# Depthwise convolution of a conformer layer: from taps spread over four engines to shifted copies multiplied on TensorE

## The chip, the cores and the metric

One Trainium2 chip, one core of it. The time is device microseconds from the start to the end of the program; the kernel before was run three times. In the profile PE is TensorE's matmul, PEld its weight load, DVE is VectorE, ACT is ScalarE, POOL is GpSimd, SP is SyncE. SPq and ACTq are the instruction streams of SP and ACT where they issue DMA transfers.

## The reference, cut to what matters

The program is four transformer layers over 256 tokens of width 1024, all float32. The second of them (the odd layer of the first block) is a convolution module followed by a mixture of experts. The part that changes is its first half:

```python
u = modulate(x, mix_pre_g, sh_m, sc_m)              # RMS norm, scale, shift: 256 x 1024
a, g = jnp.split(u @ pw1_w + pw1_b, 2, axis=-1)     # first pointwise layer, 1024 -> 2048
h = a * jax.nn.sigmoid(g)
h = depthwise_conv(h, dw_w) + dw_b                  # 31 taps along the tokens, a filter for each channel
h = jax.nn.silu(layernorm(h, ln_g, ln_b))
y = h @ pw2_w + pw2_b                               # second pointwise layer
x = x + gt_m * rmsnorm(y, mix_post_g)
```

The depthwise convolution adds, for each of 1024 channels and 256 tokens, 31 products of a tap with the value some tokens away.

## The kernel before

Weights come from HBM in pieces of 128x1024 floats (512 KB) into raw buffers, loaded by SP in the order of one long plan (class `Stream`). For a float32r product each piece is split into a rounded part and its remainder: ACT writes `hi` (L98), DVE or POOL `lo` (L99). A product is then three passes on PE, hi by hi, lo by hi, hi by lo (`mm3`, L92 to L94). There are 8 raw buffers, 10 more from the start of the second layer on, and 5 buffers each for `hi` and `lo`. The splits run ahead of the products by one chunk (two pieces).

The first pointwise layer is an exception: its 16 pieces are used as they are (`"raw"` in `conv_specs`), as plain float32 weights against the float32 input `Cu`. Channels lie on the partitions, in 8 blocks of 128; a loop of four steps makes two blocks each. For a block, PE makes the value half and the gate half (`ch`, L1059), ACT and DVE the sigmoid by tanh (`csg`, L1063 and L1064), and DVE the gated value with 15 zeros at either end (`chp`, L1068). A shifted tap is then a window of `chp`. Two tables, PE_TAPS and POOL_TAPS, say which engine computes which of the 31 taps: PE multiplies by a diagonal matrix of the tap (`diag`, L1072, built by POOL in layer 0), ACT scales a window and POOL adds it (`ctp` and `cyp`, L1082 and L1083), DVE multiplies and adds in one step (`cy`, L1086). PE turns the sums to tokens on partitions into banks of PSUM (`cyt`, L1072), where DVE takes the statistics for the layer norm (`bn`, L1096); ACT and DVE normalise into `xs` (L1107, L1109), PE turns it back (`czt`, L1119), and the second pointwise layer follows (`pz`). Behind it come a residual, the router and the experts, with weights held back by `st.pause` until the router is done.

The order of the instructions on each engine is fixed when the program is built, by a scheduler that goes by the dependences and its own estimate of times. On the chip each engine but PE's weight loads goes strictly in that order. A DMA transfer signals one of eight semaphores, used in turn by SP's and ACT's transfers, and waits for the transfer that used the same one before.

Of the kernel before, what the change touches and what calls it, by code (L numbers as in the profile page):

```python
# [21 lines left out]
T = 256  # L22
# [217 lines left out]
def rchunk(w, r0):  # L240
# [39 lines left out]
def layout(inputs):  # L280
# [5 lines left out]
    for g, names in GROUPS.items():  # L286
        a[g] = np.ascontiguousarray(np.concatenate([a.pop(k).reshape(-1, 128) for k, _ in names]).T)
    a["lambdas"] = np.concatenate([a.pop("l0_lambda_" + k) for k in ("q1", "q2", "k1", "k2")])
# [703 lines left out]

PE_TAPS = (1, 1, 3, 5, 1, 7, 5, 15)
POOL_TAPS = (13, 15, 13, 12, 11, 13, 10, 4)

LAST = (3, 6, 7)
# [9 lines left out]
def conv_diag(e, dw, pool):  # L1008

    t = pool.tile([128, sum(PE_TAPS), 128], F32, name="diag")  # L1010
    n = 0
    for cb, c in enumerate(PE_TAPS):
        for j in range(c):
            e.nc.gpsimd.tensor_tensor(t[:, n, :], e.ident, dw[:, 8 * j + cb:8 * j + cb + 1].to_broadcast([128, 128]), op=OP.mult)
            n += 1
    return t
# [19 lines left out]
def conv_mix(e, st, u, I, V, dw, diag, bias, banks, wk, wt, done, ps, z):  # L1036
# [3 lines left out]
    y = wk.tile([128, KB, T], F32, name="cy", bufs=1)  # L1040
    ba, bg = V["l1_conv_pw1_b"][:, 0:8], wk.tile([128, KB], F32, name="hbg", bufs=1)
    nc.vector.tensor_scalar(bg, V["l1_conv_pw1_b"][:, 8:16], 0.5, None, op0=OP.mult)
    p = banks.all("cyt")

    p7 = ps.tile([128, 2, 128], F32, tag="tap", name="cyt", bufs=1)
    spots = [[p[tb][cb // 4][:, 128 * (cb % 4):128 * (cb % 4) + 128] if cb < 7 else p7[:, tb, :] for cb in range(KB)]
             for tb in range(2)]
    runs = [[p[tb][0], p[tb][1][:, 0:384], p7[:, tb, :]] for tb in range(2)]
    st6 = wk.tile([128, 2, 3, 6], F32, name="bn", bufs=1)
    for i in range(4):  # L1050
        w = [st.next(), st.next()]
        for f in range(2):
            hs = ps.tile([128, 2, T], F32, tag="mm", name="ch")
            with ExitStack() as c:
                if i == 0 and f:
                    c.enter_context(e.tc.issue_after(last.ins))
                for j in range(2):
                    for k in range(KB):
                        last = nc.tensor.matmul(hs[:, j, :], w[j][k // 4][:, k % 4, 128 * f:128 * f + 128], u[:, k, :],  # L1059
                                                start=(k == 0), stop=(k == KB - 1))  # L1060
            cb = 2 * i + f
            s = wt.tile([128, T], F32, tag="csg", name="csg")
            nc.scalar.activation(s, hs[:, 1, :], AF.Tanh, bias=bg[:, cb:cb + 1], scale=0.5)  # L1063
            nc.vector.tensor_scalar(s, s, 0.5, 0.5, op0=OP.mult, op1=OP.add)  # L1064
            h = wt.tile([128, T + 2 * PAD], F32, tag="chp", name="chp", bufs=3)
            nc.gpsimd.memset(h[:, 0:PAD], 0.0)
            nc.gpsimd.memset(h[:, PAD + T:], 0.0)
            nc.vector.scalar_tensor_tensor(h[:, PAD:PAD + T], hs[:, 0, :], ba[:, cb:cb + 1], s, op0=OP.add, op1=OP.mult)  # L1068
            tap = lambda j: dw[:, 8 * j + cb:8 * j + cb + 1]
            yb = y[:, cb, :]  # L1070
            n0, n1 = PE_TAPS[cb], PE_TAPS[cb] + POOL_TAPS[cb]
            mm = lambda tb, *m, start=False, stop=False: nc.tensor.matmul(spots[tb][cb], *m, start=start, stop=stop,  # L1072
                                                                          skip_group_check=True)
            for j in range(n0):
                for tb in range(2):
                    mm(tb, h[:, 128 * tb + j:128 * tb + j + 128], diag[:, sum(PE_TAPS[:cb]) + j, :],
                       start=(j == 0 and (cb in (0, 4) or cb == 7 and tb == 0)))
            yp = wt.tile([128, T], F32, tag="cyp", name="cyp")
            nc.scalar.activation(yp, h[:, n0:n0 + T], AF.Identity, bias=V["l1_conv_dw_b"][:, cb:cb + 1], scale=tap(n0))
            for j in range(n0 + 1, n1):  # L1080
                t = wt.tile([128, T], F32, tag="ctp", name="ctp", bufs=4)
                nc.scalar.activation(t, h[:, j:j + T], AF.Copy, scale=tap(j))  # L1082
                nc.gpsimd.tensor_tensor(yp, yp, t, op=OP.add)  # L1083
            nc.vector.tensor_scalar(yb, h[:, n1:n1 + T], tap(n1), None, op0=OP.mult)
            for j in range(n1 + 1, TAPS):
                nc.vector.scalar_tensor_tensor(yb, h[:, j:j + T], tap(j), yb, op0=OP.mult, op1=OP.add)  # L1086
            parts = [yb, yp]
            if cb < 6:
                nc.vector.tensor_tensor(yb, yb, yp, op=OP.add)
                parts = [yb]  # L1090
            for tb in range(2):
                for q in parts:
                    mm(tb, q[:, 128 * tb:128 * tb + 128], e.ident, stop=(q is parts[-1]))
                if cb in LAST:
                    k = LAST.index(cb)
                    nc.vector.bn_stats(st6[:, tb, k, :], runs[tb][k])  # L1096
# [7 lines left out]
    for c, cs in enumerate((slice(0, 512), slice(512, 896), slice(896, 1024))):  # L1104
        for tb in range(2):
            if tb != (c == 2):
                nc.scalar.activation(z[:, tb, cs], runs[tb][c], AF.Identity, bias=nm[:, tb:tb + 1], scale=r[:, tb:tb + 1])  # L1107
            else:
                nc.vector.tensor_scalar(z[:, tb, cs], runs[tb][c], mv[:, tb, 0:1], r[:, tb:tb + 1],  # L1109
                                        op0=OP.subtract, op1=OP.mult)  # L1110
# [808 lines left out]
class Model:  # L1919
# [187 lines left out]
    def consts1(self, work):  # L2107
# [5 lines left out]
        load_cols(e, self.V, self.I, "vd", q, e.nc.scalar)  # L2113
        self.diag = conv_diag(e, self.V["l1_conv_dw_w"], q)
# [8 lines left out]
    def odd(self):  # L2123
# [6 lines left out]
        with ExitStack() as c2:  # L2130
# [3 lines left out]
            dw, diag, bias = V["l1_conv_dw_w"], self.diag, self.bias  # L2134
            wtc = ExitStack()
            wt = wtc.enter_context(tc.tile_pool(name="wkt", bufs=2))
            U = wt.tile([128, KB, T], F32, name="Cu", bufs=1)
            banks = Banks(psy)
            g, sh = self.gain(mod[1, 0][:, 8:16], V["l1_mix_pre_g"], "gc"), mod[1, 0][:, 0:8]
            for tb in range(2):  # L2140
# [3 lines left out]
            with tc.issue_after(act.ins):  # L2144
                gtb = self.gate_row(mod[1, 1][:, 0:8], V["l1_mix_post_g"], wk, "gtb")
# [180 lines left out]
```

## Time and profile before

| | |
|---|---|
| median of 3 runs | 1992.06 us (1989.18 to 1993.62) |
| profiled execution | 2003.04 us, its span 2001.3 us |
| PE busy | 1834.0 us, 92% |
| DVE busy | 1590.6 us, 79% |
| ACT busy | 1192.3 us, 60% |
| POOL busy | 520.9 us, 26% |
| granted TensorE clock, mean | 0.942 |
| HBM read | 465.10 MB, 233 GB/s over the span |

The span is from the first to the last instruction, the profiled time also has what lies around it. A share of the whole span is a mean over stages with different bounds, so the stage with the convolution (about 580 to 696 us) has to be read by itself. [...] One plain float32 product on PE shows as two records.

### The profile page before, as it was taken

The numbers are of one execution on the slowest core, as the hardware profiler recorded it, in microseconds if no ns is written. First come the engines' busy times: TensorE is split into PE (matmuls) and PEld (weight loads), VectorE is DVE, ScalarE is ACT, GpSimd is POOL, SyncE is SP. The second block draws the span as 40 slices with busy tenths as digits, with TensorE's granted clock in tenths as the row PEclk, the third lists the DMA queues.
The fourth block names the chain that finished last, engine by engine and source line by source line (L and its number), as shares of the span: only waits on it lengthen the run. The fifth ranks groups of instructions, "written<-read, shape, count | busy, mean of one in ns | idle before, by whom it ended". The sixth has DMA issues, their size and how long they took to land. (4 is left out here: it accounts for less than half of the span.)

```text
span 2001.3 us, 33220 instructions
## 1 busy us (share of the span) xinstructions
PE 1834.0 (92%) x12339; PEld 1636.7 (82%) x12339; DVE 1590.6 (79%) x2343; ACT 1192.3 (60%) x1844; POOL 520.9 (26%) x460
## 2 busy tenths in 40 slices
PE   6789988699998679999999999999999689989997
PEld 3678677689976569999999999999998689878896
DVE  5887898677559858999999999999998595569555
ACT  5455455455445447777777777777776544345443
POOL 1645564533227631000000000000000433335051
PEclk9889899799999889999999999999999789889799
DMA  9846676289763227999999999999996232233220
GB/s 362 286 163 211 211 229 234 81 314 322 247 215 106 79 85 268 368 347 333 348 365 349 333 350 362 353 333 345 367 350 232 95 116 96 69 126 133 81 75 22
DMA packets 132463, 468.41 MB, mean 234 GB/s; under 512 B 14994, under 2 KB 16274, under 8 KB 132292
## 3 DMA queue, kind: packets, MB, share of 16 engines
q1 hardware_dynamic: 131008, 464.38, 65.0%
q8 instruction: 99, 1.62, 0.3%
q10 hardware_dynamic: 1172, 1.65, 0.2%
q14 instruction: 72, 0.59, 0.1%
q0 software_dynamic: 112, 0.17, 0.1%
HBM read 465.10 MB, written 1.05 MB: 233 GB/s over the span
## 5 line engine op out<-in xcount | busy, mean ns | idle before, releaser
L99 DVE TENSOR_TENSOR lo<-raw,hi 128x1024 fp32r<-128x1024 f32 x678 | 858.1, 1281 | 137.2 <-ACT hi L98 112.7
L98 ACT CAST hi<-raw 128x1024 fp32r<-128x1024 f32 x718 | 746.3, 1048 | 298.3 <-PE ph L94 92.4
L93 PE MATMUL ph<-lo,gh 128*128 128x256 f32 x1408 | 396.5, 282 | 3.5 <-DVE lo L99 1.7
L94 PE MATMUL ph<-hi,gl 128*128 128x256 f32 x1408 | 396.2, 282 | 0.0
L92 PE MATMUL ph<-hi,gh 128*128 128x256 f32 x1408 | 393.7, 280 | 0.0
L93 PEld LDWEIGHTS ph<-lo,gh 128*128 128x128 f32 x1408 | 264.2, 188 | 12.6 <-DVE lo L99 6.8
L94 PEld LDWEIGHTS ph<-hi,gl 128*128 128x128 f32 x1408 | 264.2, 188 | 3.4
L92 PEld LDWEIGHTS ph<-hi,gh 128*128 128x128 f32 x1408 | 264.4, 188 | 2.8
L343 POOL TENSOR_TENSOR adac<-adac,raw 128x512 f32<-128x512 f32 x112 | 196.9, 1783 | 173.5 <-ACT raw L341 100.0
L1613 POOL MEMSET kv<- 64x2 f32 x4 | 0.4, 97 | 790.3 <-DVE lo L99 773.7
L99 POOL TENSOR_TENSOR lo<-raw,hi 128x1024 fp32r<-128x1024 f32 (+1 forms) x40 | 97.4, 2443 | 158.6 <-ACT hi L98 149.5
L93 PE MATMUL pe<-lo,hhi 128*128 128x512 f32 x352 | 137.8, 392 | 0.0
L92 PE MATMUL pe<-hi,hhi 128*128 128x512 f32 x352 | 136.8, 396 | 0.5 <-ACT hhi L98 0.5
L94 PE MATMUL pe<-hi,hlo 128*128 128x512 f32 x352 | 125.8, 392 | 0.0
L94 PE MATMUL ht<-hi,Hl 128*128 128x256 f32 (+1 forms) x384 | 115.1, 300 | 0.0
L92 PE MATMUL ht<-hi,Hh 128*128 128x256 f32 (+1 forms) x384 | 114.5, 298 | 0.6 <-ACT u L459 0.6
L93 PE MATMUL ht<-lo,Hh 128*128 128x256 f32 (+1 forms) x384 | 114.6, 298 | 0.0
L92 PE MATMUL ph<-Fh,hi 128*128 128x256 f32 x352 | 101.4, 290 | 11.5 <-DVE h L980 8.9
L93 PE MATMUL ph<-Fl,hi 128*128 128x256 f32 x352 | 101.1, 288 | 0.0
L94 PE MATMUL ph<-Fh,lo 128*128 128x256 f32 x352 | 100.1, 287 | 0.0
L1083 POOL TENSOR_TENSOR cyp<-cyp,ctp 128x256 f32<-128x256 f32 x83 | 72.4, 883 | 36.4 <-ACT ctp L1082 32.8
L92 PEld LDWEIGHTS ph<-Fh,hi 128*128 128x128 f32 x352 | 68.2, 195 | 14.5 <-DVE h L980 9.1
(598 smaller groups left out, 4115.9 us busy)
## 6 DMA issues: line engine op xcount, KB each, us to landing
raw<-in_l_moe_w SPq DMA_DIRECT2D x528, 512.0 KB, 5.4
raw<-in_l_mod_w SPq DMA_DIRECT2D x96, 512.0 KB, 5.4
raw<-in_l_ffn_w SPq DMA_DIRECT2D x66, 512.0 KB, 4.5
raw<-in_w_in SPq DMA_DIRECT2D x60, 512.0 KB, 3.6
raw<-in_w_ada SPq DMA_DIRECT2D x32, 512.0 KB, 5.0
raw<-in_l_w_in SPq DMA_DIRECT2D x28, 512.0 KB, 4.9
raw<-in_l_conv_pw_w SPq DMA_DIRECT2D x24, 512.0 KB, 4.5
raw<-in_w_ada SPq DMA_DIRECT2D x32, 256.0 KB, 3.7
```

Source lines behind the costliest of these rows:

```text
L92: mm(out, a[0], b[0], start=start, stop=False, **kw)
L93: mm(out, a[0], b[1], start=False, stop=False, **kw)
L94: return mm(out, a[1], b[0], start=False, stop=stop, **kw)
L98: nc.scalar.copy(hi, src)
L99: (lo_eng or nc.vector).tensor_tensor(lo, src, f32(hi), op=OP.subtract)
L343: nc.gpsimd.tensor_tensor(a[:, 1, i:i + 512], a[:, 1, i:i + 512], y[:, i:i + 512], op=OP.add)
L1083: nc.gpsimd.tensor_tensor(yp, yp, t, op=OP.add)
L1613: nc.gpsimd.memset(kv[64:128, :, T - 1:T], 0.0)
```

## The change

The split among engines is gone. The first pointwise layer's weights are split like all others and multiplied in three passes against a split input (`Ch`, `Cl`). That input is made by `modulate_tb`, which the other layers use already: ACT copies each group of four transposed blocks out of PSUM, DVE casts it and subtracts; the intermediate goes into the buffer `cy` through a small class `Parts`.

For the convolution each block's `chp` (now with 15 and 17 zeros) is copied within SBUF by 16 transfers issued by ACT: for each of four groups `c` of 32 channels and each of four shifts `s`, the 32 partitions of group `c` go to the partitions 32s to 32s+31 of a tile `cx4`, shifted by `s` tokens (32x284 floats, 36 KB). One product with K of 128 then adds four taps of 32 channels: the weights `cD` are 128x32, four diagonal matrices one below the other. Eight such products in a row, each shifted by four tokens, make the 32 taps (the last is zero), and the four groups write to their own 32 rows of one PSUM tile `cc`. POOL builds `cD` from a table of taps laid out on the host and four stacked identities. ACT copies `cc` out with the bias added (`cy`), PE turns it (`cyt`), ACT copies that to `xs`, and the statistics are taken there in four parts. The convolution of a pair of blocks (`convolve`) is written after the next pair's pointwise product.

```diff
 def conv_specs(pw1, pw2):
-        s += [(kchunk(pw1[4 * j + i])[0], "raw") for j in range(2)]
+        s += [kchunk(pw1[4 * j + i]) for j in range(2)]
...
+def conv_taps(e, I, pool):
+    t = pool.tile([128, 256], F32, name="taps")
+    nc.scalar.dma_start(t, I["taps"])
+    d = pool.tile([128, 32], F32, name="id4")
...
+    def convolve(i, xs):
+        p = banks.tile([128, 2, T], F32, name="cc")
+        for f, (x, d) in enumerate(xs):
+            for a in range(8):
+                for c in range(4):
+                    nc.tensor.matmul(p[32 * c:32 * c + 32, f, :], d[:, 8 * c + a, :], x[:, c, 4 * a:4 * a + T],
+                                     start=(a == 0), stop=(a == 7), skip_group_check=True)
+            nc.scalar.activation(y[:, 2 * i + f, :], p[:, f, :], AF.Identity, bias=V["l1_conv_dw_b"][:, 2 * i + f:2 * i + f + 1])
+        q = banks.tile([128, 2, T], F32, name="cyt")
+        for f in range(2):
+            for tb in range(2):
+                nc.tensor.transpose(q[:, tb, 128 * f:128 * f + 128], y[:, 2 * i + f, 128 * tb:128 * tb + 128], e.ident)
+        nc.scalar.copy(z[:, :, 256 * i:256 * i + 256], q)
+        for tb in range(2):
+            nc.vector.bn_stats(st6[:, tb, i, :], q[:, tb, :])
+
+    pend = None
     for i in range(4):
-        w = [st.next(), st.next()]
+        hs = [ps.tile([128, 2, T], F32, tag="mm", name="ch") for _ in range(2)]
+        for j in range(2):
+            w = st.next()
+            for k in range(KB):
+                for f in range(2):
+                    e.mm3(hs[f][:, j, :], w(k, 128 * f, 128), (u[0][:, k, :], u[1][:, k, :]), start=(k == 0), stop=(k == KB - 1))
+        if pend:
+            convolve(*pend)
...
+            d = wt.tile([128, 32, 32], F32, tag="cD", name="cD", bufs=2)
+            nc.gpsimd.tensor_tensor(d, taps[1][:, None, :].to_broadcast([128, 32, 32]),
+                                    taps[0][:, 32 * cb:32 * cb + 32, None].to_broadcast([128, 32, 32]), op=OP.mult)
...
+            h = wt.tile([128, T + 32], F32, tag="chp", name="chp", bufs=3)
...
+            x = wt.tile([128, 4, n], F32, tag="cx4", name="cx4", bufs=3)
+            for s in range(4):
+                for c in range(4):
+                    nc.scalar.dma_start(x[32 * s:32 * s + 32, c, :], h[32 * c:32 * c + 32, s:s + n])
+            xs.append((x, d))
+        pend = i, xs
+    convolve(*pend)
...
             for tb in range(2):
-                for k in range(0, KB, 4):
-                    p = banks.tile([128, 4, 128], F32, name="pt")
-                    act = modulate_bank(e, self.xs, tb, k, g, sh, p, U[:, k:k + 4, 128 * tb:128 * tb + 128], k == 0)
+                last = modulate_tb(e, self.xs, tb, g, sh, U, Parts(y, 512), lambda: banks.tile([128, 1, 512], F32, name="pt")[:, 0, :])
```

ACT's order from the first gated value (`csg`) on, before; `cyp` and `ctp` are the scaled windows that POOL adds:

```order
L1063 ACTIVATE csg<-ch,hbg 128x256
L1079 ACTIVATE cyp<-chp,vc,vd 128x256
L1082 ACTIVATE ctp<-chp,vd 128x256 x10
L1063 ACTIVATE csg<-ch,hbg 128x256
L1082 ACTIVATE ctp<-chp,vd 128x256 x2
L1079 ACTIVATE cyp<-chp,vc,vd 128x256
```

And now, from the same place to the second pair's first copies:

```order
L1076 ACTIVATE csg<-ch,hbg 128x256
L98 CAST hi<-raw 128x1024
L1076 ACTIVATE csg<-ch,hbg 128x256
L1085 DMA cx_5708<-chp 32x284 x16
L1085 DMA cx_5734<-chp 32x284 x16
L98 CAST hi<-raw 128x1024
L1050 ACTIVATE cy<-cc,vc 128x256
L1076 ACTIVATE csg<-ch,hbg 128x256 x2
L98 CAST hi<-raw 128x1024 x3
L1085 DMA cx_5957<-chp 32x284 x6
L1050 ACTIVATE cy<-cc,vc 128x256
L1085 DMA cx_5957<-chp 32x284 x5
```

The scaled windows are gone; in their place 32 transfers stand in a row in ACT's stream, with one weight split, the copy of the convolved block and the next pair's tanh behind them. The 16 pieces of the first pointwise layer are numbers 0 to 15 of these splits: the three ahead of the first row here are 5 to 7, then come 8, 9 (behind the transfers) and 10 to 12, with four pieces to a pair.

PE's order where the second pair's product ends and the first pair's convolution begins, now:

```order
L94 MATMUL ch<-Ch,lo 128x256
L1048 MATMUL cc<-cx_5708,cD 32x256 x32
L1048 MATMUL cc<-cx_5734,cD 32x256 x32
L1054 MATMUL cyt<-ident,cy 128x128 x2
L92 MATMUL ch<-Ch,hi 128x256
```

A block's 32 products stand together, and the next pair's product is behind both blocks of the pair before.

DVE's order at the end of layer 0, before, in the residual that leads to the changed stage (`rt`, `x`, `xs`):

```order
L927 TENSOR_TENSOR rt<-py,gtb 128x512 x2
L84 TENSOR_SCALAR r1v<-r1s 128x1
L927 TENSOR_TENSOR rt<-py,gtb 128x512
L931 SCALAR_TENSOR_TENSOR x<-rt,r1y,x 128x512 x2
L927 TENSOR_TENSOR rt<-py,gtb 128x512
```

The same place now, with the same steps under their new line numbers:

```order
L99 TENSOR_TENSOR lo<-raw,hi 128x1024
L929 TENSOR_TENSOR rt<-py,gtb 128x512 x2
L84 TENSOR_SCALAR r1v<-r1s 128x1
L929 TENSOR_TENSOR rt<-py,gtb 128x512
L372 TENSOR_TENSOR mod_1_676<-bg,vc 128x8
L933 SCALAR_TENSOR_TENSOR x<-rt,r1y,x 128x512 x2
L376 TENSOR_SCALAR mod_1_676<-mod_1_676 128x8
L99 TENSOR_TENSOR lo<-raw,hi 128x1024
L929 TENSOR_TENSOR rt<-py,gtb 128x512
L84 TENSOR_SCALAR r1v<-r1s 128x1
L99 TENSOR_TENSOR lo<-raw,hi 128x1024
```

Three subtractions of weight splits stand in and around the residual now, where there were none; the three copies of the same splits stand on ACT beside it. The order of the expert stage is as before; in the feed-forward part of layer 0 and in the last two layers some instructions have changed places.

## Rows read from the trace of the kernel before

**Rows 1.** Timeline of PE, start of the stage.
```profile
580.83 8.73 PE L1059 MATMUL ch<-Cu,raw 128*128 128x256 f32 x30
...
589.83 6.21 PE L1059 MATMUL ch<-Cu,raw 128*128 128x256 f32 x28
```

**Rows 2.** Timeline, end of the stage: start us, us, instruction.
```profile
693.33 0.39 PE L1072 MATMUL cyt<-ident,cyp 128*128 128x128 f32 x2
693.75 0.30 DVE L1096 BATCH_NORM_STATS2 bn<-cyt 128x6 f32<-128x128 f32 x1 [0.53 <-PE cyt L1072]
...
696.38 0.63 PE L1119 MATMUL czt<-ident,xs 128*128 128x128 f32 x4 [2.67 <-ACT xs L1107]
```

**Rows 3.** Busy us of PE, PEld, DVE, ACT, POOL; granted clock, DMA share, GB/s, by stretch.
```profile
592.00:680.00 88.00, 64.60 (x315) 55.39 (x314) 86.97 (x129) 47.31 (x97) 66.91 (x88) 0.91 0.38 126
680.00:696.00 16.00, 12.84 (x95) 12.46 (x94) 11.16 (x27) 3.16 (x7) 6.64 (x6) 0.87 0.00 0
765.00:1500.00 735.00, 731.56 (x5212) 682.81 (x5211) 687.73 (x748) 568.84 (x694) 1.67 (x1) 1.00 0.96 351
```

**Rows 4.** Costliest groups, 580 to 696 us: count, busy us, mean ns, idle before.
```profile
L1086 DVE SCALAR_TENSOR_TENSOR cy<-chp,vd,cy 128x256 f32<-128x256 f32 x111 | 73.5, 696 | 1.1
L1083 POOL TENSOR_TENSOR cyp<-cyp,ctp 128x256 f32<-128x256 f32 x83 | 72.4, 883 | 36.4 <-ACT ctp L1082 32.8
```

**Rows 5.** Timeline of ACT, start of the stage.
```profile
578.56 1.50 ACT L459 ACTIVATE Cu<-pt,mod,gc 128x128 f32<-128x128 f32 x4 [1.28 <-PE pt L453]
...
590.51 0.48 ACT L1063 ACTIVATE csg<-ch,hbg 128x256 f32<-128x256 f32 x1
```

**Rows 6.** One tile's subtractions: ns min/median/max, first and last start.
```profile
L99 DVE TENSOR_TENSOR cTl<-cs,cTh x4: 683/689/693, 700.0 to 711.1; 128x512 fp32r<-128x512 f32 x4
```

**Rows 7.** Page, part 5: splits of weights, count, busy us, mean ns.
```profile
L99 DVE TENSOR_TENSOR lo<-raw,hi 128x1024 fp32r<-128x1024 f32 x678 | 858.1, 1281 | 137.2 <-ACT hi L98 112.7
L98 ACT CAST hi<-raw 128x1024 fp32r<-128x1024 f32 x718 | 746.3, 1048 | 298.3 <-PE ph L94 92.4
...
L99 POOL TENSOR_TENSOR lo<-raw,hi 128x1024 fp32r<-128x1024 f32 (+1 forms) x40 | 97.4, 2443 | 158.6 <-ACT hi L98 149.5
```

**Rows 8.** Timeline of PE in layer 0's feed-forward part.
```profile
506.88 0.28 PE L93 MATMUL ph<-Fl,hi 128*128 128x256 f32 x1
507.00 0.28 PE L94 MATMUL ph<-Fh,lo 128*128 128x256 f32 x1
507.20 1.06 PE L357 MATMUL adap<-adac,ones 128*32 128x512 f32 x6
508.19 0.50 PE L92 MATMUL py<-hi,hhi 128*128 128x512 f32 x1
```

**Rows 9.** Stretch of the stage's start, columns as in rows 3.
```profile
581.00:592.00 11.00, 11.00 (x46) 9.31 (x45) 1.42 (x5) 2.94 (x8) 0.00 (x0) 0.82 0.95 372
```

**Rows 10.** Timeline of DVE, start of the stage.
```profile
591.02 0.29 DVE L1064 TENSOR_SCALAR csg<-csg 128x256 f32<-128x256 f32 x1 [9.44 <-ACT csg L1063]
591.42 0.48 DVE L1068 SCALAR_TENSOR_TENSOR chp<-ch,vc,csg 128x256 f32<-128x256 f32 x1
```

**Rows 11.** Timeline of ACT, its first two transfers.
```profile
0.80 0.89 ACTq L1906 DMA_DIRECT2D x<-in_x  x2
```

**Rows 12.** Line L1603, issue ns min/median/max, and landing.
```profile
L1603 ACTq DMA_DIRECT2D cw<-in_cmp_w x4: 482/570/1672, 1565.6 to 1787.1; - x4
...
DMA to landing us min/median/max: 1.9/2.0/2.2
```

**Rows 13.** Line L164, the weight loads: issue ns, and landing.
```profile
L164 SPq DMA_DIRECT2D raw<-in_l_moe_w x528: 327/328/702, 580.1 to 1516.0; - x176
...
DMA to landing us min/median/max: 2.6/5.2/11.0
```

**Rows 14.** Timeline of PE, four 32-row products of 256 columns.
```profile
565.84 0.63 PE L357 MATMUL adap<-adac,ones 128*32 128x256 f32 x4
566.39 0.50 PE L92 MATMUL py<-hi,hhi 128*128 128x512 f32 x1
```

More of the change, by code (lines that the diff above doesn't have):

```diff
@@ L287, in layout @@
         a[g] = np.ascontiguousarray(np.concatenate([a.pop(k).reshape(-1, 128) for k, _ in names]).T)
+    w = np.concatenate([a.pop("l1_conv_dw_w"), np.zeros((1, D), np.float32)])
+    a["taps"] = np.ascontiguousarray(w.reshape(8, 4, 8, 4, 32).transpose(1, 4, 2, 3, 0)).reshape(128, 256)
     a["lambdas"] = np.concatenate([a.pop("l0_lambda_" + k) for k in ("q1", "q2", "k1", "k2")])
@@ L989 @@
 PAD = 15
-PE_TAPS = (1, 1, 3, 5, 1, 7, 5, 15)
-POOL_TAPS = (13, 15, 13, 12, 11, 13, 10, 4)
-LAST = (3, 6, 7)
 def conv_specs(pw1, pw2):
@@ L1003, in conv_specs @@
     for i in range(4):
-        s += [(kchunk(pw1[4 * j + i])[0], "raw") for j in range(2)]
+        s += [kchunk(pw1[4 * j + i]) for j in range(2)]
     return s + [rchunk(pw2, 256 * i) for i in range(4)]
[L1008 to L1016, printed above, removed]
+def conv_taps(e, I, pool):
+    nc = e.nc
+    t = pool.tile([128, 256], F32, name="taps")
+    nc.scalar.dma_start(t, I["taps"])
+    d = pool.tile([128, 32], F32, name="id4")
+    nc.gpsimd.tensor_tensor(d, e.ident[:, 0:32], e.ident[:, 32:64], op=OP.add)
+    for i in (64, 96):
+        nc.gpsimd.tensor_tensor(d, d, e.ident[:, i:i + 32], op=OP.add)
+    return t, d
 def conv_bias(e, I, pool, work):
@@ L1033, in conv_bias, with conv_mix @@
     return one, b
-def conv_mix(e, st, u, I, V, dw, diag, bias, banks, wk, wt, done, ps, z):
+def conv_mix(e, st, u, I, V, taps, bias, banks, wk, wt, done, ps, z, y):
     nc = e.nc
-    y = wk.tile([128, KB, T], F32, name="cy", bufs=1)
     ba, bg = V["l1_conv_pw1_b"][:, 0:8], wk.tile([128, KB], F32, name="hbg", bufs=1)
     nc.vector.tensor_scalar(bg, V["l1_conv_pw1_b"][:, 8:16], 0.5, None, op0=OP.mult)
[L1043 to L1049, printed above, removed]
-    for i in range(4):
-        w = [st.next(), st.next()]
-        for f in range(2):
[L1053 to L1060, printed above, removed]
@@ L1067, in conv_mix @@
             nc.gpsimd.memset(h[:, PAD + T:], 0.0)
[L1068 to L1096, printed above, removed]
+            nc.vector.scalar_tensor_tensor(h[:, PAD:PAD + T], hs[f][:, 0, :], ba[:, cb:cb + 1], s, op0=OP.add, op1=OP.mult)
@@ L1103, in conv_mix @@
     nc.vector.scalar_tensor_tensor(nm, mv[:, :, 0], -1.0, r, op0=OP.mult, op1=OP.mult)
-    for c, cs in enumerate((slice(0, 512), slice(512, 896), slice(896, 1024))):
+    for cs in (slice(0, 512), slice(512, 1024)):
         for tb in range(2):
-            if tb != (c == 2):
-                nc.scalar.activation(z[:, tb, cs], runs[tb][c], AF.Identity, bias=nm[:, tb:tb + 1], scale=r[:, tb:tb + 1])
-            else:
-                nc.vector.tensor_scalar(z[:, tb, cs], runs[tb][c], mv[:, tb, 0:1], r[:, tb:tb + 1],
-                                        op0=OP.subtract, op1=OP.mult)
+            if tb:
+                nc.scalar.activation(z[:, tb, cs], z[:, tb, cs], AF.Identity, bias=nm[:, tb:tb + 1], scale=r[:, tb:tb + 1])
+            else:
+                nc.vector.tensor_scalar(z[:, tb, cs], z[:, tb, cs], mv[:, tb, 0:1], r[:, tb:tb + 1], op0=OP.subtract, op1=OP.mult)
     py = banks.all("pz")
@@ L2112, in consts1 @@
         self.moe = Moe(e, self.I, p)
-        load_cols(e, self.V, self.I, "vd", q, e.nc.scalar)
-        self.diag = conv_diag(e, self.V["l1_conv_dw_w"], q)
+        self.taps = conv_taps(e, self.I, q)
         self.bias = conv_bias(e, self.I, q, work)
@@ L2133, in odd @@
             ps = c2.enter_context(tc.tile_pool(name="psc", bufs=2, space=PSUM))
-            dw, diag, bias = V["l1_conv_dw_w"], self.diag, self.bias
+            taps, bias = self.taps, self.bias
             wtc = ExitStack()
             wt = wtc.enter_context(tc.tile_pool(name="wkt", bufs=2))
-            U = wt.tile([128, KB, T], F32, name="Cu", bufs=1)
+            U = tuple(wt.tile([128, KB, T], F32R, name=n, bufs=1) for n in ("Ch", "Cl"))
             banks = Banks(psy)
             g, sh = self.gain(mod[1, 0][:, 8:16], V["l1_mix_pre_g"], "gc"), mod[1, 0][:, 0:8]
+            y = wk.tile([128, KB, T], F32, name="cy", bufs=1)
             for tb in range(2):
-                for k in range(0, KB, 4):
-                    p = banks.tile([128, 4, 128], F32, name="pt")
-                    act = modulate_bank(e, self.xs, tb, k, g, sh, p, U[:, k:k + 4, 128 * tb:128 * tb + 128], k == 0)
-            with tc.issue_after(act.ins):
+                last = modulate_tb(e, self.xs, tb, g, sh, U, Parts(y, 512), lambda: banks.tile([128, 1, 512], F32, name="pt")[:, 0, :])
+            with tc.issue_after(last[0].ins):
                 gtb = self.gate_row(mod[1, 1][:, 0:8], V["l1_mix_post_g"], wk, "gtb")
             st.pause(self.moe_start + 3)
-            py, room = conv_mix(e, st, U, I, V, dw, diag, bias, banks, wk, wt, wtc.close, ps, self.xs)
+            py, room = conv_mix(e, st, U, I, V, taps, bias, banks, wk, wt, wtc.close, ps, self.xs, y)
             residual(e, x, py, gtb, wk, "r2", self.xs, room)
```

12 lines of the change are left out of this document (10 added, 2 removed), and 1 row of the table GROUPS.

## The prediction

> **What bounds the kernel now.** I read the busy times by stretch first, then the costliest groups and the waits of the one stretch that the change rewrites, then its two ends in the timeline. The changed stage begins at 580.83 us with the first pointwise product [rows 1] and ends at 696.38 us, when PE starts turning the normalised result [rows 2]. In between VectorE is the bound: busy 87.0 of 88.0 us from 592 to 680, while PE has 64.6 and ScalarE 47.3 [rows 3]. The groups say with what: 111 tap steps of 696 ns on DVE, 73.5 us, beside 83 additions on POOL for another 72.4 us [rows 4]. DMA moves nothing from 680 to 696, so the weight buffers of the expert stage are full before the stage is over. From 765 to 1500 the expert stage is then full on both PE (731.6 of 735) and DMA (351 GB/s) [rows 3]. Hence every microsecond by which 696.38 moves shows in the total: the transfers ahead are as far as the buffers let them be either way, and no stage behind has room to take it up.
>
> **What goes.** All tap work on DVE, POOL and ACT, and with it the bound; PE's 38 diagonal taps go too. Late next is a chain through three engines, so the new end has to be built step by step, on the clock of the trace before. I call the four steps of the loop pairs 0 to 3 (two blocks of 128 channels each).
>
> **The start.** The modulated input is now copied by ACT alone, four groups of 1.50 us from 578.56 [rows 5], each followed on DVE by a cast and a subtraction; a 128x512 subtraction takes 0.69 us [rows 6], and I take the cast at the same. The first products read the third group: 578.56 + 4.50 + 1.38 = 584.4. Three weight splits now stand between the residual's steps. They cost nothing if they fill its gaps, and 3 x (1.05 + 1.28) = 7.0 us if none does [rows 7]; I take 2, since DVE and ACT alternate there. Start: 586.5, against 580.83.
>
> **The pointwise product.** One pair is 96 float32r passes (2 x 8 x 2 x 3) at 0.12 us [rows 8], 11.5 us. [...] Pair 0 ends at 586.5 + 13.6 = 600.1. Then tanh (0.48) on ACT, two steps on DVE (0.29 + 0.48) [rows 5, 10] and 0.3 to hand on: the first block's copies can be issued at 601.7. Pair 1's product starts at 602.5, when both accumulators are read, and ends at 614.0.
>
> **The copies.** Sixteen transfers of 36 KB a block, all issued by ACT, 32 a pair, 128 in all. This is the step with the widest price. ACT's two transfers of [rows 11] take 0.89 us together, 0.45 each; the four 32 KB ones of [rows 12] have an issue of 0.48 to 1.67, median 0.57; a weight load's issue on SP is down to 0.33 [rows 13]. I take 0.45, the only pair that ACT issued with nothing else between, and keep 0.33 and 0.60 as bounds. A 32 KB transfer lands after 1.9 to 2.2 us, median 2.0 [rows 12]. Every transfer waits for the one eight places earlier, and 8 x 0.45 = 3.6 us is more than 2.0, so that wait is covered; it ceases to be when landing takes over 3.6, as the weight loads do (5.2 median, [rows 13]). Pair 0: 32 x 0.45 = 14.4, issued by 616.1, landed by 618.1.
>
> **The taps on PE.** A block is 8 steps of four products, each into its own 32 rows. Four such products of 512 columns took 0.99 us to the next instruction (507.20 to 508.19), with different data each [rows 8]; of 256 columns 0.55 us [rows 14]. In a stream the step is thus between 0.44 (the difference) and 0.55; I take 0.47, so 3.8 us a block (3.5 to 4.4).
>
> **One round.** Pair 0's first block: 614.0 to 617.8. Its second waits for its copies: 618.1 to 621.9. On ACT stand in a row, behind the 32 issues: one weight split (1.05), the copy out of the first block (0.45), two tanh (0.96), then 1.2 of DVE, so pair 1's copies start 2.8 us after the first block's end: 620.6. They take 14.4, plus 1 us in which the copy of the transposed result, placed among them, waits for PE, plus 2.0 to land: a round of 2.8 + 17.4 = 20.2 us from first block to second block of the next pair. PE's own path is 3.8 + 11.5 + 0.5 + 3.8 = 19.6. The two are nearly equal; the copies lead by 0.6. The weights come in time: a pair's third and fourth splits stand ahead of its copies, only the second half of the pair after next is behind them. The splits add 16 x 1.28 on DVE and 16 x 1.05 on ACT [rows 7], with DVE otherwise nearly empty. POOL builds the tap weights, 128x1024 each, at about 2.4 us (the nearest is its subtraction [rows 7]); two are ready beforehand and the others have a round each.
>
> **The end.** The first blocks end at 617.8, 637.7 and 657.6; the last copies start at 660.4, are issued at 675.8 and landed at 677.8. PE then has nothing but the last two blocks: the first runs from 670.6 to 676.5 (3.8 + 2.1 for the clock), the second from 677.8 to 681.6. Behind it: copy with bias (0.65), transposes (0.35), copy and statistics (2.0), then the unchanged 2.3 us from the last statistics (694.05) to 696.38 [rows 2]. Sum 3.0 + 2.3 = 5.3: 686.9, against 696.38, so 9.5 us earlier. The 38 diagonals that POOL no longer builds in layer 0, and the reordering of some instructions in the last two layers, I put at +0.5 together, between -3 and +3. Net -9.
>
> The profiled execution took 2003.04 us, 1.74 around its span of 2001.3. So the sum is 2003.04 - 9 = 1994, and the median of the three runs stands 10.98 lower: 1992.06 - 9 = **1983 us**.
>
> **Rivals.**
> 1. *ACT's issue becomes the bound* (0.25). If one issue costs 0.60, nearer to the median of [rows 12], pair 0's copies end at 620.9, a round on ACT is 32 x 0.60 + 1 + 3.7 = 23.9, the last copies start at 672.4 and land at 694.6, and the end is 703.7: 7 us later, 1999; with the full 7 us of splits at the start 2004. By straight line the sign turns at 0.53 us an issue. For it: the 1.67 of [rows 12], issued while weights were loading. Against it: only about four weight loads fall into each round.
> 2. *The gain is lost at the start* (0.13). Splits, cast and cold clock put the first product at 593, and the reordered later stages add a little: 1990, no change.
> 3. *The four products of a step run one after another* (0.02), so the change does not do what it says. A block costs 15.2, and the end is 614.0 + 4 x 30.4 + 2 x 12 + 5.3 = 765: 2061. [rows 8, 14] speak plainly against it.
> 4. *Small transfers do not overlap* (0.02). At 2.0 us each, one after another, four pairs take 4 x 64 + 3 x 3.7: an end near 878, 2174. Against it: 512 KB weight loads land after 5.2 us but follow at 351 GB/s, one in 1.5 us [rows 3, 13], so several are under way at once. [...]
> 5. *The issues hide* (0.02), because ACT's issuing runs beside its computing. At nothing an issue, the last copies land at 661.8, right behind pair 2, and the end is 661 + 7.6 + 5.3 = 674: 22 us early, 1970. Against it: in [rows 11] the issues follow one another, 0.89 us for two, and here 32 stand in line with nothing long to hide under. [...]
>
> **How the numbers follow.** My forecast has 0.56, with its own range 1978 to 1988: at an issue of 0.33 the end is 13.3 us early, and 15 with no cost for the splits (1977). To 1974 with all small terms on the good side, and up to 2003, which takes in rival 2 and most of rival 1, leaves under 2 in 10 outside (rivals 3 to 5, the worst of rival 1). A measurement here tells 0.2%, 4 us, from no change. Faster by more: 0.53 of mine, 0.03 of rival 2, 0.01 of rival 1, 0.02 of rival 5: 0.59. Within: 0.03 + 0.08 + 0.03 = 0.14. Slower: 0.21 + 0.02 + 0.04 = 0.27.
>
> **What would show it.** ACT's 128 issues about 0.45 us apart with no wait between them; four products of a step starting together, steps 0.47 apart; first blocks some 20 us apart; a pause on PE of 8 to 10 us before the last pair; the turn of the normalised result at 687. I am wrong if the issues are over 0.53 apart, or if they stop for weight loads; then ACT's queue, not PE, is where the splits and copies stand late.

## The result and the profile after

The change makes the kernel slower: 2011.03 us median (2002.48 to 2032.53, 20 runs) against 1996.82 us (1987.66 to 2004.24, 20 runs), ratio 1.0087 with a 95% interval of 1.0066 to 1.0108. The forecast was 1983 us, 9 us faster, from the 1992.06 of the first three runs of before. (The ratios are taken from undisturbed runs alone, so they are not the quotient of the medians.) The profiled execution took 2021.83 us, its span 2019.9 us.

The stretches of [rows 3] in the changed kernel, with the same columns:

```profile
592.00:680.00 88.00, 64.61 (x685) 57.37 (x684) 22.74 (x35) 19.62 (x30) 12.23 (x16) 0.88 0.43 128
680.00:706.00 26.00, 13.97 (x133) 7.99 (x134) 2.04 (x8) 2.09 (x4) 0.70 (x1) 0.79 0.12 33
```

DVE has gone from 87.0 of 88 us to 22.7, POOL from 66.9 to 12.2. ACT's busy time fell too, from 47.3 to 19.6, and PE's is the same. No engine is the bound by its busy time, and yet the stage ends later. What fills it is not counted as busy: in the 88 us ACT spends 65.0 on issuing copies, beside its 19.6. ACT's timeline shows it; ACTq is ACT where it issues transfers, and in brackets stands its idle time before the row:

```profile
593.03 0.48 ACT L1076 ACTIVATE csg<-ch,hbg 128x256 f32<-128x256 f32 x1
593.08 21.52 ACTq L1085 DMA_DIRECT2D cx<-chp  x32
614.63 1.04 ACT L98 CAST hi<-raw 128x1024 fp32r<-128x1024 f32 x1 [21.12 <-DMA cx<-chp]
615.59 0.47 ACT L1050 ACTIVATE cy<-cc,vc 128x256 f32<-128x256 f32 x1
615.96 0.83 ACT L1076 ACTIVATE csg<-ch,hbg 128x256 f32<-128x256 f32 x2
```

The 32 copies of the first pair take ACT 21.5 us, and the split, the copy of the convolved block and the next pair's tanh come only then. The line of the copies by itself (ns of one issue, min, median, max; then first and last start, and who waited):

```profile
L1085 ACTq DMA_DIRECT2D cx<-chp x128: 514/602/1623, 593.1 to 693.9; - x128
...
  POOL chp L1079: 55.7, 5
  ACT hi L98: 47.3, 3
  ACT cy L1050: 16.7, 1
  ACT xs L1055: 10.3, 2
  PE cc L1048: 6.0, 1
...
DMA to landing us min/median/max: 1.8/1.9/6.6
```

An issue takes 0.602 us, and from one start to the next it is 0.641 (median of the 127 distances). Landing takes 1.9 us, as forecast from [rows 12]. The stage's end on PE:

```profile
683.12 7.12 PE L1048 MATMUL cc<-cx,cD 128*32 128x256 f32 x64 [6.03 <-DMA cx<-chp]
695.17 1.29 PE L1048 MATMUL cc<-cx,cD 128*32 128x256 f32 x6 [4.93 <-ACT cy L1050]
...
705.86 1.14 PE L1110 MATMUL czt<-ident,xs 128*128 128x128 f32 x4 [3.41 <-DVE xs L1101]
```

Before each of its last two blocks PE stands idle for 6.0 and 4.9 us, and the blocks then run at a granted clock of 0.63 and 0.73. These are means, as is the 0.79 of the stretch: the trace records the clock as 0.50 or 1.00 of full speed. The normalised result is turned at 705.86, against 696.38 [rows 2].

To see where the rest of the time went, every traced kernel is cut at the same products. "FFN 0" is the feed-forward part of layer 0 (first `ph` to last `py`), "start" from there to the first pointwise product `ch`, "stage" from it to the first `czt`, "experts" from the first expert product `ph` to the last `pe`, "last layers" from there to the last `hy`. All in us.

| kernel | FFN 0 | start | stage | experts | last layers |
|---|---|---|---|---|---|
| before | 210.9 | 8.6 | 115.6 | 793.8 | 442.7 |
| before, second trace (e12) | 210.8 | 8.6 | 113.0 | 795.8 | 435.1 |
| changed | 202.4 | 16.5 | 128.2 | 797.8 | 448.2 |
| e1: copies issued by SP | 199.2 | 16.5 | 120.2 | 798.4 | 439.9 |
| e2: copies on DVE | 198.7 | 16.5 | 98.3 | 797.8 | 445.3 |
| e3: three passes, old taps | 211.1 | 14.0 | 133.7 | 797.3 | 448.8 |
| e4: new taps, raw weights | 199.1 | 12.1 | 128.5 | 798.4 | 435.8 |
| e6: copies through HBM | 199.8 | 16.5 | 90.4 | 797.8 | 439.6 |
| e7: half as many transfers | 199.7 | 16.6 | 92.0 | 798.4 | 440.1 |
| e8: copies on DVE and ACT | 202.4 | 16.5 | 88.1 | 797.3 | 454.6 |
| e9: changed, diagonals built again | 200.3 | 16.5 | 128.0 | 797.9 | 430.2 |
| e10: e8, order at the experts' head | 205.1 | 16.5 | 88.6 | 797.5 | 441.7 |
| e11: before without the diagonals | 205.6 | 8.5 | 113.6 | 798.5 | 439.3 |

Between the first and the third row the program loses 12.7 us in the stage, 8.0 at the start and 3.9 in the experts, and wins 8.5 in FFN 0: +16.1 us. Ahead of FFN 0 stand 2.6 us less, behind the stage 0.3. The last layers add 5.6 between these two traces, but that can't be put down to the change. The changed kernel, e2, e6, e7, e8 and e9 have the same order of instructions there, and need 430 to 455 us. What differs is the clock that PE was granted in that execution (columns as in [rows 3]; first e9, then the changed kernel, then e8). The kernel before, in its own order, fits in: 435.1 us at 0.92 and 442.7 at 0.90.

```profile
1559.80:1989.90 430.10, 396.64 (x2868) 356.08 (x2868) 287.65 (x734) 198.13 (x434) 155.55 (x100) 0.93 0.29 94
```
```profile
1560.17:2008.41 448.24, 415.46 (x2869) 372.83 (x2868) 287.44 (x734) 198.66 (x434) 154.17 (x100) 0.89 0.28 90
```
```profile
1519.36:1973.91 454.55, 424.04 (x2868) 379.88 (x2868) 287.87 (x734) 198.83 (x434) 155.51 (x100) 0.86 0.28 89
```

### The profile page after: what moved, and what is told of

It reads as the page before. It is cut to its first block, busy times and chain, and to the rows that moved or that the text cites. A ratio compares the mean times of both kernels' runs of the same rounds, so it can differ in the third digit from the quotient of the medians.

```text
span 2019.9 us, 34046 instructions
## 1 busy us (share of the span) xinstructions
PE 1844.9 (91%) x12803; PEld 1645.2 (81%) x12803; DVE 1523.0 (75%) x2234; ACT 1173.2 (58%) x1788; POOL 455.2 (23%) x351
## 5 line engine op out<-in xcount | busy, mean ns | idle before, releaser
L99 DVE TENSOR_TENSOR lo<-raw,hi 128x1024 fp32r<-128x1024 f32 x694 | 871.3, 1271 | 186.4 <-ACT hi L98 166.4
L98 ACT CAST hi<-raw 128x1024 fp32r<-128x1024 f32 x734 | 762.4, 1048 | 319.3 <-PE ph L94 98.9
L92 PEld LDWEIGHTS ht<-hi,Hh 128*128 128x128 f32 x384 | 79.0, 206 | 3.5 <-issue 1.7
L93 PEld LDWEIGHTS ht<-lo,Hh 128*128 128x128 f32 x384 | 78.8, 205 | 1.7 <-issue 1.5
```

Source lines behind the costliest of these rows:

```text
L92: mm(out, a[0], b[0], start=start, stop=False, **kw)
L93: mm(out, a[0], b[1], start=False, stop=False, **kw)
L98: nc.scalar.copy(hi, src)
L99: (lo_eng or nc.vector).tensor_tensor(lo, src, f32(hi), op=OP.subtract)
```

## The experiments

**e1: who issues.** 

```diff
-                    nc.scalar.dma_start(x[32 * s:32 * s + 32, c, :], h[32 * c:32 * c + 32, s:s + n])
+                    nc.sync.dma_start(x[32 * s:32 * s + 32, c, :], h[32 * c:32 * c + 32, s:s + n])
```

> The 128 copies are issued by SP instead of ACT; nothing else is edited. Theory 1 (the changed kernel is late because ACT issues a copy every 0.64 us, 82 us in one line, with its casts and activations standing in that line; an issue costs less on SP, 0.33 us as a weight load's does): the copies of a pair take about 12 us, PE's own path sets the rounds (11.3 + 7.6 + 0.5 = 19.4 us), the normalised result is turned near 667 instead of 705.9, and the time is near 1972. Rival A (the 0.64 us belongs to this kind of transfer, 32 partitions within SBUF, on whatever queue): SP issues at 0.64 too, pairs follow one another every 20.5 us, the turn comes near 685, the time near 1991. Rival B (not the issue but the landing or the shared semaphores pace the copies): they come as late as from ACT, 2011. Rival C (the loss is not in this stage but in the later stages, whose order changed): the stage gets shorter and the time still stays above 2000.

2009.03 us, ratio to before 1.0085 (1.0045 to 1.0125). The copies' line on SP:

```profile
L1085 SPq DMA_DIRECT2D cx<-chp x128: 507/589/1622, 589.5 to 682.4; - x128
```

SP needs 0.589 us an issue, 0.633 from start to start, though it issues its weight loads in 0.33 [rows 13]. So Theory 1's "an issue costs less on SP" fell and rival A's price is right: it belongs to the kind of transfer. Rival B is out by the spacing: eight issues take 8 x 0.633 = 5.1 us, and a copy lands after 1.9 us in the median, so neither landing nor a shared semaphore paces the row. A's time was not reached. The stage is only 8 us shorter, because the copies still stand in one line, 92.9 us from the first start to the last, now with weight loads and their waits between them. In the median even those 8 us don't show, though the interval has room for them.

**e2: no transfers at all, DVE copies.**

```diff
-                    nc.scalar.dma_start(x[32 * s:32 * s + 32, c, :], h[32 * c:32 * c + 32, s:s + n])
+                    nc.vector.tensor_scalar(x[32 * s:32 * s + 32, c, :], h[32 * c:32 * c + 32, s:s + n], 1.0, None, op0=OP.mult)
```

> No transfers: each of the 128 copies of 32x284 is one instruction on DVE (multiply by 1.0), which writes to another group of 32 partitions. Theory 1 (ACT's line of issues sets the stage): a copy should take about 0.3 us (the nearest row is 0.287 us for 128x256 of the same operation), 32 of them 9.6 us a pair, with four weight splits 14.5 us, less than PE's 19.4; PE sets the rounds, the turn comes near 667 and the time near 1972. Rival B (PE's products or the splits set the stage): the turn stays near 700, 2005 to 2011. Rival C (the loss lies in the later stages): the stage gets shorter but the time stays above 2000. A miss of another kind: if a copy to other partitions costs 0.7 us, DVE has 27 us a pair and the gain is gone.

1982.53 us, ratio 0.9926 (0.9895 to 0.9957): faster than before. One line's instructions, and the stretch from the first to the last convolution, with the columns of [rows 3]:

```profile
L1085 DVE TENSOR_SCALAR cx<-chp x128: 295/300/2062, 597.4 to 671.5; 32x284 f32<-32x284 f32 x128
```
```profile
604.00:676.00 72.00, 63.86 (x758) 49.27 (x750) 64.54 (x143) 19.80 (x28) 13.66 (x14) 0.98 0.29 96
```

A copy on DVE takes 0.300 us where its transfer took 0.641 of ACT's line. The stage fell by 30 us to 98.3, not to the some 89 of Theory 1 (a turn near 667). DVE is busy 64.5 of 72 us and some of its copies take up to 2.06, but PE is at 63.9 too; that DVE is the bound here is tested by e8. Rival B is refuted, and C: the stage does reach the total. Twelve of a block's 16 copies write to another group of 32 partitions than they read; their median with the other four, 0.300 us for 284 columns, is near the 0.29 us that the same operation took for 256 columns on their own partitions [rows 10].

**e3 and e4: each part alone.** e3 is the kernel before with

```diff
-        s += [(kchunk(pw1[4 * j + i])[0], "raw") for j in range(2)]
+        s += [kchunk(pw1[4 * j + i]) for j in range(2)]
...
+                    e.mm3(hh[f][:, j, :], w(k, 128 * f, 128), (u[0][:, k, :], u[1][:, k, :]), start=(k == 0), stop=(k == KB - 1))
```

and the split input (and one buffer fewer for the scaled windows, which no run tests by itself); e4 is the changed kernel with these lines and the input as they were before.

> One part of the change alone: the first pointwise layer in three float32r passes with split weights and input, on the old convolution by taps on four engines (one buffer fewer for the scaled windows, for room). Theory 1: the old taps keep DVE the bound, and 16 subtractions of 1.28 us come on top, with cast and subtraction of the input ahead: 20 + 4 us longer, near 2020. Rival (the passes save PE time that counts, 11.3 us a pair against 14.2): faster than before, 1985 to 1990.

> The other part alone: the new convolution with its 128 transfers on ACT, the first pointwise layer with its raw float32 weights and float32 input as before the change. Theory 1 (the line of issues on ACT sets the stage): without weight splits in ACT's line a round is 20.5 + 3 us, and PE's 14.2 + 7.6 + 0.5 = 22.3 lies under it; the start is some 5 us earlier without the split of the input; the turn near 694, the time 1997 to 2001, faster than the changed kernel by about 12 us. Rival B (PE or the splits set the stage): PE's longer product makes it slower than the changed kernel, 2015 to 2020. Rival C (the order of later stages): no clear difference from 2011.

e3: 2032.93 us, ratio 1.0187 (1.0153 to 1.0221). Theory 1's mechanism holds: the stage grows by 18.2 us, near the 20.5 that 16 subtractions cost on DVE [rows 7], the start by 5.4. Its 2020 was 13 us short; in the trace the rest is in the other columns of the table and in the time before FFN 0 (6.0 us). e4: 2005.22 us, ratio 1.0056 (1.003 to 1.0083). The gain over the changed kernel is some 6 us by the medians, half of what was expected, and the two intervals overlap. In the traces the start is 4.4 us shorter (12.1 against 16.5), but the stage is as long as before the undoing: the issues are again 0.642 us apart, and where splits were taken out of ACT's line its waits for PE's longer product grew, from 8.7 us to 14.3. So neither part helps alone, and the three passes cost less inside the new stage than beside the old taps.

**e6 and e7: is it paid per transfer?** e6 goes through HBM in five transfers a block. e7 copies 64 rows at a time and leaves out that the rows belong in other places.

```diff
+    dr = e.ctx.enter_context(e.tc.tile_pool(name="hdp", bufs=3, space=bass.MemoryType.DRAM))
...
-            for s in range(4):
-                for c in range(4):
-                    nc.scalar.dma_start(x[32 * s:32 * s + 32, c, :], h[32 * c:32 * c + 32, s:s + n])
+            hd = dr.tile([128, T + 32], F32, tag="hd", name="hd", bufs=3)
+            nc.scalar.dma_start(hd, h)
+            for s in range(4):
+                nc.sync.dma_start(x[32 * s:32 * s + 32, :, :], hd[:, s:s + n].rearrange("(c p) n -> p c n", c=4))
```
```diff
-            for s in range(4):
+            for s in (0, 2):
                 for c in range(4):
-                    nc.scalar.dma_start(x[32 * s:32 * s + 32, c, :], h[32 * c:32 * c + 32, s:s + n])
+                    nc.scalar.dma_start(x[32 * s:32 * s + 64, c, :], h[64 * (c // 2):64 * (c // 2) + 64, s:s + n])
```

> A block's 16 transfers become five: ACT writes the 128x288 block to a scratch buffer in HBM, SP reads it back four times, once for each shift, 32x4x284 (128 rows) a time. Question: is the 0.64 us of an issue paid per transfer or per row? Theory 1 (per transfer, so 40 issues instead of 128, about 26 us on two queues, and some 4 us a block to write and land): the stage, 128.2 us in the changed kernel from first pointwise product to the turn of the normalised result, comes down to 95 to 102 us, the time to 1978 to 1985. Rival (per row: a read of 128 rows costs four times 0.6): 32 x 2.4 = 77 us on SP, the stage stays at 120 to 128, the time at 2005 to 2011.

> As the changed kernel, on ACT, but half as many transfers of twice the rows: 8 a block of 64x284, same bytes. It leaves the placement of the copies out: a transfer takes 64 neighbouring rows with one shift, so taps meet wrong rows. Theory 1 (an issue costs 0.64 us whatever its rows): 64 issues, 41 us in all instead of 82, a pair's copies 10.3 us; the stage 100 to 105 us instead of 128.2, the time 1985 to 1990. Rival (a cost per row or per byte): each issue about 1.2 us, the stage and the time as in the changed kernel, 2011.

e6: 1977.24 us, ratio 0.9911 (0.9877 to 0.9945). e7: 1987.9 us, ratio 0.9942 (0.9904 to 0.9979). Issue times, first e6's writes and reads, then e7's copies:

```profile
L1085 ACTq DMA_DIRECT2D hd<-chp x8: 326/326/363, 597.8 to 650.9; - x8
```
```profile
L1087 SPq DMA_DIRECT2D cx<-hd x32: 303/430/496, 600.1 to 656.1; - x32
...
DMA to landing us min/median/max: 2.6/3.8/5.4
```
```profile
L1085 ACTq DMA_DIRECT2D cx<-chp x64: 468/607/1122, 588.8 to 654.4; - x64
```

0.602 us for 32 rows, 0.607 for 64: paid per transfer, not per row. e6's copies to and from HBM are cheaper to issue, 0.326 and 0.430 us with 128 rows, though that is no rule for all such copies (the loads of [rows 12] had a median of 0.57). Why the kinds differ no run here shows. Theory 1 is confirmed by both stages (90.4 and 92.0 us, shorter than it said), though e6's copies land later (3.8 us) and need two steps. The rivals, a cost per row or per byte, are out. Against the changed kernel e6 gained 37.8 us of stage with 40 issues instead of 128, e7 36.2 with 64; what they saved was the issuing engine's time, not landing (3.8 and 2.3 us in the median, against 1.9).

**e8 and e10: is PE next?** e8 divides e2's copies, 10 of a block to DVE and 6 to ACT. e10 adds to e8 the old order at the head of the experts; the lines that hand on `m.last`, the last split of the gathered tokens, and read `st.late` are left out here.

```diff
+                    o, v = x[32 * s:32 * s + 32, c, :], h[32 * c:32 * c + 32, s:s + n]
+                    if 4 * s + c < 10:
+                        nc.vector.tensor_scalar(o, v, 1.0, None, op0=OP.mult)
+                    else:
+                        nc.scalar.copy(o, v)
```
```diff
-                oh = m.onehots(0, x)
+                with tc.issue_after(m.last[1].ins) if x else ExitStack():
+                    oh = m.onehots(0, x)
...
+            st.late = range(self.moe_start + 2, self.moe_start + 4), m.last
```

> No transfers; of a block's 16 copies DVE makes 10 (0.30 us each, as measured when DVE made all) and ACT 6. With all on DVE the stage was 98.3 us and DVE was busy 64.5 of its 72 us between first and last convolution. Theory 1 (DVE is the bound there, and PE's 19.4 us a pair comes next): the stage gets to 87 to 90 us, the time to 1971 to 1975. Rival (PE's path is already what sets it): 98, 1982, no change. Second rival (ACT's copies come late, behind its casts): over 98.

> The kernel with copies on DVE and ACT, and two issue orders at the head of the expert stage put back to what they were before the change: ACT's third to sixth weight split, and the second pair's one-hot rows on DVE, behind the last split of the gathered tokens. From the first expert product to the first turned hidden block it took 11.7 us before and 17.6 to 18.8 in all kernels with the change. Theory (in the new order POOL's subtraction starts while DVE still has one-hots and subtractions to do, and two of them take 2.6 us instead of 0.42): 11 to 14 us there, the whole stretch to the end of the experts 793 to 795 instead of 797.4, the time 4 us lower, near 1976. Rival (it comes from weights that arrive later): 17 to 19 as before.

e8: 1980.15 us, ratio 0.9883 (0.9837 to 0.9929). Its stretch from the first to the last convolution:

```profile
604.00:665.00 61.00, 55.69 (x720) 41.66 (x718) 43.42 (x87) 33.13 (x62) 13.83 (x13) 0.99 0.33 105
```

The stage is 88.1 us, where Theory 1 put it, so DVE was e2's bound. PE is now busy 55.7 of 61 us at a clock of 0.99, DVE 43.4: by busy share the bound is PE, though no run takes work from PE to test it. The prediction's sum for issues that hide (rival 5) gives a stage of 674 - 586.5 = 87.5. By its ratio e8 is ahead of before and of the changed kernel; against e2, e6, e7 and e10 the intervals overlap. Its median lies above the 1971 to 1975 expected.

e10: 1981.02 us, ratio 0.9914 (0.9879 to 0.9949), no gain over e8. What e10 is to undo was read from the changed kernel's trace, DVE at the head of the experts, where pairs of operations that take 0.75 us together took 2.9:

```profile
765.45 0.75 DVE L99 TENSOR_TENSOR gl<-gu,gh 128x256 fp32r<-128x256 f32 x2
766.80 2.93 DVE L1219 TENSOR_TENSOR oh<-slots,rt 128x256 fp32r<-128x256 f32 x2 [0.60 <-PE otp L1230]
769.65 2.90 DVE L99 TENSOR_TENSOR gl<-gu,gh 128x256 fp32r<-128x256 f32 x2
```

In e10 the one-hots take 0.75 us again, and the first hidden block is turned 9.3 us after the first expert product instead of 17.6. But the whole expert stretch is 797.5 us as in e8: what the head gained was given back behind it. So the theory is right on the stall and wrong on its worth, and the 2 to 4 us that the experts lost stay unexplained. e11 has them too (798.5), with the old convolution, and the two traces of before are themselves 2.0 us apart.

**e9, e11 and e12: the gain ahead of the stage.** 

```diff
+    g = work.tile([128, 38, 128], F32, name="diag", bufs=1)
+    for i in range(38):
+        nc.gpsimd.tensor_tensor(g[:, i, :], e.ident, t[:, i:i + 1].to_broadcast([128, 128]), op=OP.mult)
```

is e9, added to the changed kernel (one execution each for e9, e11 and e12); e11 puts `e.nc.vector.memset(t, 0.0)` in the place of the loop in `conv_diag` of the kernel before; e12 is the kernel before, unchanged.

> The changed kernel with POOL's 38 diagonal blocks of 128x128 built again in layer 0, where they were built before; nothing reads them. One look, at the feed-forward part of layer 0 (first to last product): 210.9 us before, 202.4 in the changed kernel, 198.7 to 202.4 in the three others without the diagonals and 211.1 in the one with them. Theory 1 (while POOL builds 38 diagonals in a row, DVE gets almost nothing done: one subtraction took 13.8 us beside them, and PE waited 9 us for it): 209 to 213 again, with one subtraction of over 10 us on DVE. Rival (the order of the other instructions, or the clock, made it shorter): 198 to 203.

> The kernel before, without the 38 multiplications on POOL that build the diagonals: the tile is set to zero by one instruction on DVE, so the taps of TensorE are left out of the result; its products run all the same. One look at the feed-forward part of layer 0, 210.9 us before. Putting the 38 multiplications into the changed kernel did not bring the time back (200.3 against 202.4). Theory 1 (in the order of before, the train keeps one subtraction on DVE for 13.8 us, and PE waits for the step behind it): 199 to 203 us without the train. Rival (the order of the other instructions makes it long): 208 to 212 with no such subtraction.

> The kernel before once more, unchanged, for a second trace. Theory (the differences of the feed-forward part of layer 0, of the stage and of the head of the expert stage are due to the programs, those of the last two layers to the clock of the single execution): 210 to 212 us, 115 to 116 us and 11 to 13 us again; the last two layers off from the first trace's 442.7 us by several us. Rival (all of them vary from run to run): the first three off by as much as 5 us too.

The kernel before, DVE in layer 0, and its waits there in the order line, time, times, longest:

```profile
365.33 16.31 DVE L99 TENSOR_TENSOR lo<-raw,hi 128x1024 fp32r<-128x1024 f32 x3
```
```profile
ACT hi L98 <- DMA raw<-in_l_ffn_w: 13.9, 4, 10.5
PEld ph L92 <- DVE h L980: 9.1, 1, 9.1
PE ph L92 <- DVE h L980: 8.9, 1, 8.9
```

Three subtractions of 1.28 us [rows 7] take 16.3 us there, 13.8 of them the first, while POOL builds the diagonals from 365.5 on; PE waits 8.9 us for a step of DVE that stands behind them. e3, which has the same train, shows the same 16.3 us. In e9 the train starts its multiplications from 365.0 to 385.9, and yet its longest subtraction on DVE is

```profile
376.37 4.91 DVE L99 TENSOR_TENSOR lo<-raw,hi 128x1024 fp32r<-128x1024 f32 x1 [0.51 <-ACT hi L98]
```

no longer than in the kernels without the train (3.7 to 5.4 us at the longest, 4.28 in the changed kernel). FFN 0 took 200.3 us, so the train alone does not do it: Theory 1 of e9 fell. e11, without it, needed 205.6, between the two expectations, its longest subtraction 4.23 us. So by one trace each some 5 of the 8.5 us went with the train in the order of before, and the rest is the order of the other instructions or not told apart. e12 repeats FFN 0 and the start (210.8 and 8.6 us) and the head of the experts (11.6 us, in the first trace 11.7). Its stage of 113.0 lies below the 115 to 116 expected and its experts are 2.0 us longer, so two executions of one program can differ by 2 to 3 us there; the last layers are 7.6 us off.

## Why the prediction was wrong

- **The issue price is the step that failed.** "I take 0.45" was the pair of loads in [rows 11], with 0.60 as the upper bound, just above the median of [rows 12] (0.57). Both move data from HBM; no row of the trace before showed a transfer within SBUF. It is 0.641 from start to start, outside the bounds and past the 0.53 that the prediction named as its sign of being wrong. From the first to the last issue the prediction had 73.6 us (601.7 to 675.3): 127 x 0.45 = 57.2 and 16.5 of pauses. Measured are 100.9 (593.1 to 693.9): 127 x 0.641 = 81.4 and 19.5. That is +24.2 from the price and +3 from the pauses, of a stage that came out 27.8 us longer than its 100.4.
- **Most else in the stage held, one sum by luck.** First product to first issue was 15.2 forecast, 15.45 measured. In it, and again in the seventh block, the forecast has 2.1 us for a lower clock. Why the clock is lower there no run shows; in the changed kernel the passes are 0.213 us apart at a granted clock of 0.50 up to 582.6, then 0.118 at 1.00, and the first pair's 96 passes took 14.4 us against 13.6. The four products of a step ran side by side: the first block took 3.8 us, 0.47 a step. PE's pauses before the last blocks came (8 to 10 us forecast, 6.0 and 4.9 measured), but the block behind a pause was dearer than forecast: 5.7 to 7.1 us in the five cases, against 3.8 and once 5.9; the longest, the seventh, ran at a granted clock of 0.63. From the last issue's end to the turn 11.1 was forecast and 11.3 measured because errors offset each other: the last block began 0.6 us after that issue instead of 2.0, took 6.3 us instead of 3.8 (with two transposes in between), and the rest took 4.4 instead of 5.3.
- **Rival 1 was what happened**, at a price beyond the one it was worked out with. By its own sum, in which 128 issues stand in a row, 0.64 gives an end 12.6 us late by the trace before; measured are 12.7 for the stage and 8.0 for the start, together 20.7. It had 0.25; "nearer to the median of [rows 12]" was the better reading, and the bound should have gone well past it, since the transfer was of a kind with no row.
- **Rivals 3 to 5 are out.** The products of a step overlap (eight records of 0.38 us, two for a product, in 0.47), small transfers overlap (landing 1.9 us, one every 0.64), and the issues do not hide: an issue takes a third of the 1.9 us that its copy needs to land, but the 32 of the first pair held ACT for 21.5 us.
- **The start** cost 8.0 us instead of 5.7; rival 2, with 12.2, did not come. Of it 4.4 go with the split input and weights (e4 has 12.1; alone, in e3, they cost 5.4), and 3.5 remain with raw weights. These 3.5 are a term that the prediction put at nothing: the first two blocks' tap weights were to be "ready beforehand". On POOL they stand ahead of the second half's `r1ny`, the factor of the RMS norm that the start waits for. The changed kernel, then the kernel before:

```profile
568.17 2.30 POOL L1073 TENSOR_TENSOR cD<-id,taps 128x1024 f32<-128x1024 f32 x1 [1.07 <-ACT xs L938]
570.52 1.91 POOL L1073 TENSOR_TENSOR cD<-id,taps 128x1024 f32<-128x1024 f32 x1
572.57 0.72 POOL L86 TENSOR_TENSOR r1ny<-r1nv,mhalf 128x1 f32<-128x1 f32 x1
```
```profile
577.61 0.55 POOL L86 TENSOR_TENSOR r1ny<-r1nv,mhalf 128x1 f32<-128x1 f32 x1 [0.24 <-DVE r1nv L84]
```

From the start of DVE's scaling of the first half (`xs`) to that of this `r1ny` it is 1.17 us in the four traces without `cD` and 4.62 to 4.66 in the nine with it.

- **The 38 diagonals and the reordering**, put at +0.5 together, were mis-sized: FFN 0 is 8.5 us shorter, the experts 2 to 4 longer. The stall of 13.8 us stood in the trace before, but the prediction looked at POOL's time and not at what DVE did beside it. The statement ahead of the prediction that the expert stage kept its order was wrong by two one-hots and some of the splits at its head.
- **The range** missed because its upper end, 2003, held a price of 0.60 at most, and nothing for longer experts (2 to 4 us). The price, the pauses and the start put the turn 30.1 us later than forecast; FFN 0 gave 8.5 back. Some 4.8 us of the distance to 1983 lie in its base: the 20 runs of before have 1996.82, the three before the prediction 1992.06.

## What to carry to other kernels

Before work is moved into transfers, count the transfers and multiply by the time from one issue to the next on one engine, for the kind of transfer meant: 128 x 0.64 = 82 us was more than the 73.5 us of DVE that it replaced. Where no row shows that kind, the bound must go past the dearest row of another kind, or the kind be measured first; then prefer few transfers (40 issues instead of 128 took 37.8 us off the stage), or a copy on an engine that has become free (0.30 us on DVE). Ask of work that is to be done beforehand what stands behind it on its engine: 4.2 us of tap weights on POOL made the start 3.5 us later. An engine's busy share does not show issuing (19.6 us busy beside 65.0 of issues here): read what stands behind a run of issues in the same stream.

## What was not expected of the hardware

- Issuing a copy within SBUF took 0.60 us on ACT and 0.59 on SP for 32 rows, and 0.61 on ACT for 64; SBUF to HBM took 0.33, HBM to SBUF with four groups of rows 0.43.
- A subtraction on DVE took 13.8 us instead of 1.28 beside a train of small multiplications on POOL, in three traces of one order; in another order with the same train, at most 4.9, and without a train still up to 5.4.
- The same order of instructions took 430 to 455 us for the last two layers, at a mean granted clock of 0.93 to 0.86.
